# The second layer of a Strassen MLP: steps over four quads of units instead of two, with 1024-column splits

## The chip, the cores and the metric

The kernel runs on one core of a Trainium2 chip. Times are device microseconds of one execution. The engines are PE (matmuls), DVE, ACT and POOL (elementwise work) and SP, which issues most of the DMAs. Each engine works through its own queue in order.

## The reference, cut to what matters

Depth is one, so one Conformer convolution module and one squared-ReLU MLP are computed for 2048 tokens of width 1024, in float32:

```
h = rms_norm(x, mix_norm)
a, g = split(h @ w_in + b_in);  h = a * sigmoid(g)
h = causal_depthwise_conv_31(h) + conv_b
x = x + silu(layer_norm(h, ln_g, ln_b)) @ w_out + b_out
x = x + square(relu(rms_norm(x, mlp_norm) @ w1)) @ w2      # d_ff = 4096
```

## The kernel before

Activations lie transposed (features on partitions, 512 tokens to a tile), so there are four blocks of tokens. float32 products are made of three float32r matmuls: each operand is split into a high half (an ACT cast) and a low half (a DVE or POOL subtraction), and high by high, high by low and low by high are accumulated. "A split" below is this pair of instructions.

The first part of the program (up to some 1190 us) does the convolution of all blocks and the MLP of blocks 0 and 1. Nothing in it changes but the way one address of w2 is written. The second part, after `front.close()`, opens new pools and does blocks 2 and 3:

- *Projection* (`project_spilled`, twice 8 products of 24 matmuls): the convolution's output is read back from DRAM through the tiles of `loaded`, split, and multiplied by w_out; x2, the residual stream, goes to DRAM (`x2_pairs`).
- *First MLP layer* (class `Quad`). The two token blocks and the two halves of the weights make a 2 by 2 block product, done in Winograd's form of Strassen's scheme with 7 products instead of 8. The seven forms of the activations are B11, B21, T2, T1, T3, B22 and T4; the weights' are A11, A12, S2, S1, S3, S4 and A22. A quad is 2 x 128 hidden units for both blocks; there are 16. Its products are called P1, P2, P6, P5, P7, P3 and P4, 12 matmuls each. For the first twelve quads (`EARLY`) P1 and P2 run ahead, and their results wait in DRAM. After the squared ReLU POOL makes the seven forms that the second layer needs (four subtractions a quad, L785 to L788), and SP stores them (`keep`).
- *Second MLP layer* (L857 to L902). Outer loop: groups g of two quads (NG = 8); inner loop: two halves o of the output. One (g, o) is a half step: it loads two weight tiles of 512 KB (`raw_wq`), forms the seven weight forms in 512-column pieces (`blocks`, `w_split`), and does seven products of 12 matmuls on two pairs of PSUM banks (`both`). Each of the four finished results is a pair of tiles, 512 KB, added into x2 in DRAM by an accumulating DMA that POOL issues (L882). In the last group x2 is loaded instead, added, and stored to the output. `hidden(g)` loads and splits the hidden units of a group, 14 loads of 256 KB, once for both halves; the next group's call stands after the half o = 0.

Buffers that matter: 29 activation tiles (16 + 13) of 512 columns, high and low half, taken in turn; 6 weight splits of 512 columns (`N_WQ`); 5 load buffers (`N_LD`); 6 output tiles (`N_CC`); 4 raw weight tiles of 1024 columns; 4 pairs. The tile framework orders each engine's queue by itself, by priority and by what it expects to be ready; the code above sets program order and buffers only.

## Time and profile before

| | |
|---|---|
| three runs, median (lowest to highest) | 1991.04 us (1986.84 to 1992.85) |
| profiled execution: time, span | 1986.6, 1984.8 us |
| mean granted PE clock | 0.981 |
| busy: PE, PEld, DVE, ACT, POOL | 95%, 78%, 81%, 42%, 29% |
| DMA moved, mean rate | 303.15 MB, 153 GB/s |
| q0 (accumulating DMAs, issued by POOL) | 29.36 MB, 8.3% of 16 engines |
| q1 (all other DMAs, issued by SP) | 272.28 MB, 41.2% of 16 engines |

PE stands for the matmuls; their records overlap, so 95% doesn't mean that PE runs at its peak. PEld is the loading of weights into it. The share of a queue is the time that its packets took on the sixteen DMA engines.

### The profile page before, as it was taken

The numbers are of one execution on the slowest core, as the hardware profiler recorded it, in microseconds if no ns is written. First come the engines' busy times: TensorE is split into PE (matmuls) and PEld (weight loads), VectorE is DVE, ScalarE is ACT, GpSimd is POOL, SyncE is SP. The second block draws the span as 40 slices with busy tenths as digits, with TensorE's granted clock in tenths as the row PEclk, the third lists the DMA queues.
The fourth block names the chain that finished last, engine by engine and source line by source line (L and its number), as shares of the span: only waits on it lengthen the run. The fifth ranks groups of instructions, "written<-read, shape, count | busy, mean of one in ns | idle before, by whom it ended". The sixth has DMA issues, their size and how long they took to land.

```text
span 1984.8 us, 23561 instructions
## 1 busy us (share of the span) xinstructions
PE 1889.5 (95%) x8192; PEld 1544.2 (78%) x8192; DVE 1609.1 (81%) x2364; ACT 824.7 (42%) x1336; POOL 585.2 (29%) x387
## 2 busy tenths in 40 slices
PE   8999999999999999999999998999999998888897
PEld 6888888888778878788888876878888876766775
DVE  7999999999999999789999844785888586666653
ACT  5323225243453333443222424464445664555541
POOL 2256322644445630000000003402666421111113
PEclk9999999999999999999999998999999999999998
DMA  5223221432223333552221448856765598888875
GB/s 199 64 86 111 98 77 65 143 102 96 85 83 126 127 107 117 181 180 95 66 70 59 143 165 282 266 179 221 240 227 207 174 270 215 219 214 211 210 156 172
DMA packets 141623, 303.15 MB, mean 153 GB/s; under 512 B 13632, under 2 KB 40384, under 8 KB 141504
## 3 DMA queue, kind: packets, MB, share of 16 engines
q1 hardware_dynamic: 133440, 272.28, 41.2%
q0 software_dynamic: 8064, 29.36, 8.3%
q8 instruction: 64, 1.05, 0.2%
q14 instruction: 55, 0.45, 0.1%
HBM read 210.12 MB, written 91.47 MB: 152 GB/s over the span
## 4 chain that ended last, share of the span: by engine, by line
PE 39%; DMA 10%; DVE 5%; issue 3%; ACT 2%; POOL 0%; SPq 0%; DVEq 0%; ACTq 0%; POOLq 0%
PE ps L163 16%; PE px L609 11%; PE pz L609 5%; PE px L163 4%; DMA rawq<-in_w 4%; PE py L609 2%; DMA ld<-hB 2%; DMA ld<-hT 2%; DVE wq L585 1%; DVE act L93 1%; DMA c<-x 1%; ACT act L92 1%; ACT wq L584 0%; DMA x<-c 0%; DMA c<-conv 0%
## 5 line engine op out<-in xcount | busy, mean ns | idle before, releaser
L163 PE MATMUL ps<-act,w 128*128 128x512 f32 x2880 | 666.8, 392 | 10.2 <-ACT w L92 7.8
L163 PEld LDWEIGHTS ps<-act,w 128*128 128x128 f32 x2880 | 542.1, 189 | 126.7 <-ACT w L92 7.8
L163 PE MATMUL ps<-hid,w 128*128 128x512 f32 x1920 | 445.9, 392 | 6.2 <-DVE hid L93 5.8
L163 PEld LDWEIGHTS ps<-hid,w 128*128 128x128 f32 x1920 | 360.4, 189 | 86.8 <-DVE hid L93 8.6
L609 PE MATMUL px<-act,wq 128*128 128x512 f32 x1536 | 381.3, 402 | 44.1 <-DVE p L871 30.2
L609 PEld LDWEIGHTS px<-act,wq 128*128 128x128 f32 x1536 | 297.0, 195 | 114.5 <-DVE p L871 33.8
L352 DVE SCALAR_TENSOR_TENSOR cacc<-hc,cw,cacc 128x512 f32<-128x512 f32 x464 | 324.6, 748 | 1.4
L352 DVE SCALAR_TENSOR_TENSOR cacc<-h,cw,cacc 128x512 f32<-128x512 f32 x464 | 316.8, 747 | 0.0
L93 POOL TENSOR_TENSOR w<-raw,w 128x1024 fp32r<-128x1024 f32 x90 | 218.1, 2424 | 287.2 <-ACT w L92 281.3
L92 ACT CAST w<-raw 128x1024 fp32r<-128x1024 f32 (+1 forms) x150 | 155.1, 1035 | 289.3 <-PE ps L163 284.7
L609 PE MATMUL pz<-act,wq 128*128 128x512 f32 x768 | 186.7, 392 | 4.7 <-ACT p L828 2.8
L585 DVE TENSOR_TENSOR wq<-rawq,wq 128x512 fp32r<-128x512 f32 x144 | 116.3, 815 | 74.4 <-ACT wq L584 74.2
L609 PEld LDWEIGHTS pz<-act,wq 128*128 128x128 f32 x768 | 145.4, 190 | 36.0 <-ACT p L828 3.3
L584 ACT CAST wq<-rawq 128x512 fp32r<-128x512 f32 x192 | 117.8, 620 | 124.1 <-DMA rawq<-in_w_out 39.1
L585 POOL TENSOR_TENSOR wq<-rawq,wq 128x512 fp32r<-128x512 f32 x48 | 71.5, 1491 | 192.4 <-ACT wq L584 176.5
L440 DVE TENSOR_TENSOR h<-h,ps 128x512 f32<-128x512 f32 x128 | 86.9, 683 | 31.2 <-PE ps L163 29.5
L427 ACT ACTIVATE relu<-ps 128x512 f32<-128x512 f32 x64 | 38.2, 597 | 161.1 <-PE ps L163 160.9
L163 PE MATMUL px<-act,wq 128*128 128x512 f32 x384 | 90.2, 396 | 8.5 <-ACT act L92 7.9
L93 DVE TENSOR_TENSOR act<-ld,act 128x512 fp32r<-128x512 f32 x112 | 79.2, 726 | 23.5 <-ACT act L92 23.0
L609 PE MATMUL py<-act,wq 128*128 128x512 f32 x384 | 93.8, 392 | 2.9 <-DVE cc L697 2.9
L163 PEld LDWEIGHTS px<-act,wq 128*128 128x128 f32 x384 | 73.4, 192 | 24.8 <-ACT act L92 8.4
L882 POOL DMA_DIRECT2D x<-p x28 | 24.4, 872 | 230.3 <-DVE p L871 221.8
(133 smaller groups left out, 1816.7 us busy)
## 6 DMA issues: line engine op xcount, KB each, us to landing
raw<-in_w SPq DMA_DIRECT2D x104, 512.0 KB, 3.6
rawq<-in_w SPq DMA_DIRECT2D x76, 512.0 KB, 4.9
xt<-in_xT SPq DMA_DIRECT2D x64, 256.0 KB, 3.6
ld<-hT SPq DMA_DIRECT2D x64, 256.0 KB, 5.4
raw<-in_w_in SPq DMA_DIRECT2D x30, 512.0 KB, 3.2
x<-p POOLq DMA_DIRECT2D x28, 512.0 KB, 6.8
hB<-cc SPq DMA_DIRECT2D x48, 256.0 KB, 2.8
ld<-hB SPq DMA_DIRECT2D x48, 256.0 KB, 5.1
```

The costliest lines, as they stand in the source:

```text
L92: nc.scalar.copy(hl[:, 0, :], src)
L93: eng.tensor_sub(hl[:, 1, :], src, hl[:, 0, :].bitcast(F32))
L163: nc.tensor.matmul(ps, lhsT=w(k, a), rhs=x[:, b, :], start=k == 0 and i == 0, stop=k == len(xs) - 1 and i == 2,)
L352: nc.vector.scalar_tensor_tensor(out, h[:, k : k + T], cw[:, j, k : k + 1], acc, ALU.mult, ALU.add)
L427: nc.scalar.activation(r, ps, AF.Relu)
L440: nc.vector.tensor_add(x2[i][m], x2[i][m], ps)
L584: nc.scalar.copy(hl[:, 0, :], src)
L585: eng.tensor_sub(hl[:, 1, :], src, hl[:, 0, :].bitcast(F32))
L609: nc.tensor.matmul(ps, lhsT=hl[:, a, off + k * P : off + (k + 1) * P], rhs=x[:, b, :], start=first and k == 0 and i == 0, stop=k == n - 1 ...
L882: nc.gpsimd.dma_start(at, c, accum_op=ALU.add)
```

## The change

The second layer takes four quads a step, so there are 4 steps of two halves instead of 8. A product is 24 matmuls (`both` lists the four addresses in the weight tile), and the outputs are accumulated in DRAM after 3 steps instead of 7: 24 accumulating DMAs instead of 56. The forms of four quads lie together in DRAM (`hid_d`), so a load brings two quads, 512 KB; it is split as one tile of 1024 columns by one cast and one subtraction (`Split.add_pair`). A half step has four weight tiles, each split whole. Weight splits are all made by DVE. The buffers are cut anew: 14 activation pairs of twice the size, 2 weight splits of 1024 columns and 4 of 512, 3 load buffers ("in", which also hold C11 and P1 of a quad, `ca`) and 2 output tiles ("out"), 4 mid tiles and 2 sum tiles of 1024 columns. In the last step x2 is added when P1, P6, P5 and P4 are evicted (`kept`, `base`). The descriptor space of the accumulating DMAs is 4096 instead of 8192.

```diff
-N_WQ, N_LD, N_CC = 6, 5, 6
+N_LD = {"in": 3, "out": 2}
...
-    n_act = {"low": 16, "high": 13}
...
+    def act_pair(name="act"):
+
+        n = taken[0] % 14
         taken[0] += 1
...
+        side, pool_, bufs = ("high", high, 6) if n < 6 else ("low", low, 8)
+        return pool_.tile([P, 2, 2, T], F32R, name=name, tag=side, bufs=bufs)
+
+    class Split:
...
+        def add_pair(self, src):
+            t = act_pair()
+            self.pairs.append([t, 2])
+            nc.scalar.copy(t[:, 0], src)
+            nc.vector.tensor_sub(t[:, 1], src, t[:, 0].bitcast(F32))
...
     def mid_tile(name):
-        return mid.tile([P, T], F32, name=name, tag="m", bufs=6)
+        return mid.tile([P, T], F32, name=name, tag="m", bufs=4)
...
+    def w_split(src, eng=nc.vector):
+
+        n = src.shape[-1]
+        tag, bufs = ("wq", 2) if n == 2 * T else ("wh", 4)
+        hl = wts.tile([P, 2, n], F32R, name="w", tag=tag, bufs=bufs)
+        nc.scalar.copy(hl[:, 0, :n], src)
+        eng.tensor_sub(hl[:, 1, :n], src, hl[:, 0, :n].bitcast(F32))
         return hl
...
+    def sum_tile(name):
+        return mid.tile([P, 2 * T], F32, name=name, tag="s", bufs=2)
+
+    def wide(name, tag="out"):
+        return wts.tile([P, 2, T], F32, name=name, tag=tag, bufs=N_LD[tag])
...
-    hid_d = [{n: dram.tile([P, T], F32, name=f"h{n}_{q}") for n in form} for q in range(NQ)]
+    hid_d = [{n: dram.tile([P, 4, T], F32, name=f"h{n}_{g}") for n in form} for g in range(NQ // 4)]
...
         def p2(self):
             y = ybank()
-            product(y, w_split(self.a1[:, T:], nc.vector), form["B21"])
-            self.c11 = squared_relu(added(y, self.c1))
+            self.product(y, self.w12, "B21")
+            self.ca = wide("ca", "in")
+            self.c11 = squared_relu(added(y, self.c1, self.ca[:, 0, :]))
...
         def p3(self):
-            product(self.z, w_split(self.s4, nc.gpsimd), form["B22"], first=False)
-            self.c12 = squared_relu(added(self.z, self.u2))
+            self.product(self.z, self.ws4, "B22", first=False)
+            self.c12 = squared_relu(added(self.z, self.u2, self.cb[:, 1, :]))
...
     def hidden(g):
         out = {}
-        for n in (b for _, b in ORDER):
-            out[n] = [act_split(loaded(hid_d[2 * g + k][n])) for k in range(2)]
+        for n in ORDER:
+            s = Split()
+            for k in range(0, 4, 2):
+                s.add_pair(loaded(hid_d[g][n][:, k : k + 2, :]))
+            out[n] = s.parts()
         return out
 
     def blocks(g, o):
-        a1, a2 = [raw_wq(w2[g, o][:, 2 * i : 2 * i + 2]) for i in range(2)]
...
+        a11, a12, a21, a22 = [raw_wq(w2[g, o][:, i]) for i in range(4)]
+        s1, s2 = sum_tile("s1"), sum_tile("s2")
+        yield w_split(a11)
+        yield w_split(a12)
         nc.vector.tensor_add(s1, a21, a22)
         nc.vector.tensor_sub(s2, s1, a11)
-        out["S2"] = w_split(s2, nc.vector)
...
+            product(ps, w, hs, [k // 2 * T + i * 2 * P + k % 2 * P for k in range(4)], first)
...
+    steps = NG // 2
     h = hidden(0)
-    for g in range(NG):
+    for g in range(steps):
...
+            def out(x, n, t, ts=()):
+                for i, ps in enumerate(ts):
+                    nc.vector.tensor_add(t[:, i, :], ps, t[:, i, :])
                 if not end:
-                    nc.gpsimd.dma_start(at, c, accum_op=ALU.add)
+                    nc.gpsimd.dma_start(x2_pairs[n][2 * o + x], t, accum_op=ALU.add)
+                    return
...
             ws = blocks(g, o)
             px, py, pz = [[f() for _ in range(2)] for f in (xbank, ybank, zbank)]
-            both(px, "P1", h["B11"], ws["A11"])
-            p1 = copied(px, "p1")
...
+            w = [next(ws) for _ in range(3)]
+            both(px, h["B11"], w[0])
+            p1 = kept(px, "p1", 0, 0)
+            w.append(next(ws))
+            both(py, h["B21"], w[1])
+            out(0, 0, p1, py)
...
-    nc = bacc.Bacc("TRN2", target_bir_lowering=False, num_devices=1, dynamic_dma_scratch_size=8192)
+    nc = bacc.Bacc("TRN2", target_bir_lowering=False, num_devices=1, dynamic_dma_scratch_size=4096)
```

Three places of the queues. First SP at the start of the projection, where the first product's eight inputs (s, from conv_0) and the weights (rawq) are loaded; before:

```order
L590 DMA rawq<-in_w_out 128x1024
L598 DMA s<-conv_0_112 128x512
L598 DMA s<-conv_0_114 128x512
L598 DMA s<-conv_0_116 128x512
L598 DMA s<-conv_0_118 128x512
L598 DMA s<-conv_0_120 128x512
L590 DMA rawq<-in_w_out 128x1024
L598 DMA s<-conv_0_122 128x512
L598 DMA s<-conv_0_124 128x512
L598 DMA s<-conv_0_126 128x512
```

and with the change:

```order
L613 DMA rawq<-in_w_out 128x1024
L626 DMA s<-conv_0_112 128x512
L626 DMA s<-conv_0_114 128x512
L626 DMA s<-conv_0_116 128x512
L613 DMA rawq<-in_w_out 128x1024 x2
L626 DMA s<-conv_0_118 128x512
L626 DMA s<-conv_0_120 128x512
L626 DMA s<-conv_0_122 128x512
L613 DMA rawq<-in_w_out 128x1024
L626 DMA s<-conv_0_124 128x512
L626 DMA s<-conv_0_126 128x512
```

Three inputs instead of five stand ahead of the first wait for a buffer, and two weight tiles go between the third and the fourth.

Second, SP at the end of the first layer. The names hB and hT are the stored forms; with the change 10090 and 10091 are B11 and B21 of the first group, 10094 is T2, and 10111 to 10117 are the seven of the last group. Before, loads of the first quads' forms are already between the stores of quads 14 and 15:

```order
L598 DMA ld<-hT_0_10154 128x512
L712 DMA hB_14_10251<-cc 128x512
L598 DMA ld<-hT_1_10161 128x512
L598 DMA ld<-hT_0_10156 128x512
L598 DMA ld<-hT_1_10163 128x512
L590 DMA rawq<-in_w 128x1024
L598 DMA ld<-hB_0_10153 128x512
L712 DMA hT_14_10252<-h_12872 128x512
L712 DMA hT_14_10253<-h_12873 128x512
L712 DMA hT_14_10254<-cc 128x512
L712 DMA hB_15_10256<-cc 128x512
```

With the change T2 of the first group follows the last store of the last quad:

```order
L626 DMA ld<-hB_0_10090 128x1024
L626 DMA ld<-hB_0_10091 128x1024
L749 DMA hB_3_10113<-cb 128x512
L626 DMA ld<-hB_0_10091 128x1024
L749 DMA hT_3_10114<-h_12648 128x512
L749 DMA hB_3_10112<-ca 128x512
L749 DMA hT_3_10115<-h_12649 128x512
L749 DMA hT_3_10116<-cb 128x512
L749 DMA hT_3_10117<-h_12650 128x512
L626 DMA ld<-hT_0_10094 128x1024 x2
```

The loads have moved behind the stores that wait for POOL.

Third, DVE in a second half (o = 1) of the second layer, where act<-ld is a split of hidden units, w or wq one of a weight form, s a sum, and p, u are evictions. Before:

```order
L871 TENSOR_TENSOR p_14726<-py,p_14726 128x512
L93 TENSOR_TENSOR act<-ld,act 128x512 x2
L871 TENSOR_TENSOR p_14726<-py,p_14726 128x512
L585 TENSOR_TENSOR wq<-rawq,wq 128x512
L93 TENSOR_TENSOR act<-ld,act 128x512
L842 TENSOR_TENSOR s_15037<-rawq 128x512
L93 TENSOR_TENSOR act<-ld,act 128x512
L843 TENSOR_TENSOR s_15038<-s_15037,rawq 128x512
L585 TENSOR_TENSOR wq<-rawq,wq 128x512
L93 TENSOR_TENSOR act<-ld,act 128x512
L848 TENSOR_TENSOR rawq<-rawq,s_14825 128x512
```

With the change:

```order
L910 TENSOR_TENSOR rawq<-rawq,s_13045 128x1024
L573 TENSOR_TENSOR act<-ld,act 128x1024 x2
L608 TENSOR_TENSOR w<-s_13045,w 128x1024
L943 TENSOR_TENSOR p_13081<-py,p_13081 128x512
L573 TENSOR_TENSOR act<-ld,act 128x1024
L943 TENSOR_TENSOR p_13081<-py,p_13081 128x512
L573 TENSOR_TENSOR act<-ld,act 128x1024
L608 TENSOR_TENSOR w<-s_13044,w 128x1024
L573 TENSOR_TENSOR act<-ld,act 128x1024 x2
L608 TENSOR_TENSOR w<-rawq,w 128x1024
L573 TENSOR_TENSOR act<-ld,act 128x1024 x2
```

Each split covers 1024 columns, and two splits of hidden units stand ahead of each weight split.

## Rows read from the trace of the kernel before

**Rows 1.** Windows, 1198 to 1976 us: busy us and instructions of each engine, clock, DMA share, GB/s.

```profile
1198.00:1290.00 92.00, 91.05 (x395) 74.95 (x396) 55.72 (x78) 43.81 (x75) 42.02 (x30) 0.97 0.84 277
1290.00:1340.00 50.00, 47.13 (x211) 38.55 (x210) 43.35 (x78) 34.16 (x62) 2.70 (x2) 1.00 0.54 180
1340.00:1594.00 254.00, 254.00 (x1122) 210.08 (x1120) 186.10 (x213) 133.88 (x227) 137.23 (x92) 1.00 0.64 214
1594.00:1603.20 9.20, 7.30 (x26) 5.78 (x26) 6.66 (x11) 7.20 (x14) 0.00 (x0) 0.81 0.96 321
1603.20:1975.80 372.60, 325.68 (x1345) 261.93 (x1343) 231.84 (x365) 181.76 (x329) 68.59 (x70) 0.94 0.81 206
```

**Rows 2.** PE timeline: start us, us, engine line op tiles xcount [idle before <-releaser].

```profile
1198.36 0.80 PE L163 MATMUL px<-act,wq 128*128 128x512 f32 x1 [7.94 <-ACT act L92]
...
1600.45 5.60 PE L609 MATMUL px<-act,wq 128*128 128x512 f32 x24
...
1973.03 2.88 PE L609 MATMUL px<-act,wq 128*128 128x512 f32 x12
```

**Rows 3.** Lines by form, 1606 to 1985 us: count | busy us, mean ns | idle before.

```profile
L609 PE MATMUL px<-act,wq 128*128 128x512 f32 x757 | 196.7, 415 | 44.1 <-DVE p L871 30.2 <-ACT p L828 4.9 <-DVE c L873 4.7
...
L609 PE MATMUL pz<-act,wq 128*128 128x512 f32 x384 | 92.8, 390 | 2.8 <-ACT p L828 2.8
```

**Rows 4.** Chain of waits, 1600 to 1985 us: start us, us, what.

```profile
1680.63 2.72 PE py L609 x12
...
1751.28 10.47 DMA rawq<-in_w
...
1797.35 11.63 DMA rawq<-in_w
```

**Rows 5.** Queues and issues, 1600 to 1985 us: packets, MB, share; count, KB, us to landing.

```profile
q0 software_dynamic: 8064, 29.36, 42.9%
q1 hardware_dynamic: 21904, 49.57, 37.6%
...
rawq<-in_w SPq DMA_DIRECT2D x29, 512.0 KB, 7.3
x<-p POOLq DMA_DIRECT2D x28, 512.0 KB, 6.8
ld<-hT SPq DMA_DIRECT2D x54, 256.0 KB, 5.7
...
c<-x SPq DMA_DIRECT2D x8, 512.0 KB, 4.2
```

**Rows 6.** Instructions of tile ld, 1600 us to the end.

```profile
DMA to landing us min/median/max: 2.5/6.1/11.9
```

**Rows 7.** DVE and ACT timelines near 1148 us, splits of 1024 columns.

```profile
1148.48 1.23 DVE L93 TENSOR_TENSOR w<-raw,w 128x1024 fp32r<-128x1024 f32 x1 [0.94 <-ACT w L92]
...
1147.41 1.04 ACT L92 CAST w<-raw 128x1024 fp32r<-128x1024 f32 x1
```

**Rows 8.** SP and ACT timelines at the hand-over.

```profile
1192.03 2.66 SPq L598 DMA_DIRECT2D s<-conv  x5
...
1199.72 1.52 SPq L598 DMA_DIRECT2D s<-conv  x3
...
1202.41 1.27 ACT L92 CAST act<-s 128x512 fp32r<-128x512 f32 x2
```

**Rows 9.** Lines of POOL (1350 to 1600 us) and of DVE (1350 to 1550 us).

```profile
L585 POOL TENSOR_TENSOR wq<-rawq,wq 128x512 fp32r<-128x512 f32 x32 | 48.7, 1521 | 98.0 <-ACT wq L584 85.2 <-DMA p<-p 6.5 <-DVE cc L697 4.1
L788 POOL TENSOR_TENSOR h<-cc,h 128x512 f32<-128x512 f32 x15 | 25.1, 1672 | 9.6 <-DVE s L723 6.2 <-ACT cc L702 1.6 <-DVE wq L585 1.2
...
L585 DVE TENSOR_TENSOR wq<-rawq,wq 128x512 fp32r<-128x512 f32 x20 | 24.9, 1251 | 11.8 <-ACT wq L584 11.8
```

**Rows 10.** Chain of waits, the last 11 us.

```profile
1973.98 4.64 DMA c<-x
1978.74 0.69 DVE c L873
```

More of the change, by code (lines that the diff above doesn't have):

```diff
@@ L627, in load_plain @@
         raw = raw_wq(src)
-        hl = [w_split(raw[:, h * T : (h + 1) * T], (nc.vector, nc.gpsimd)[h]) for h in range(2)]
-        return lambda k, a: hl[k // 4][:, a, k % 4 * P : (k % 4 + 1) * P]
+        hl = w_split(raw)
+        return lambda k, a: hl[:, a, k * P : (k + 1) * P]
     def project_spilled(b, ss, norm, w0=None):
@@ L649, in conformer_mlp @@
     HK = KD // 2
-    form = {n: [None] * HK for n in ("B11", "B21", "B22", "T1", "T2", "T3", "T4")}
+    form = {n: Split() for n in ("B11", "B21", "B22", "T1", "T2", "T3", "T4")}
     n0 = [None] * HK
@@ L709, in __init__, with kept, product @@
             self.q, self.early = q, False
+        def kept(self, n):
+            return hid_d[self.q // 4][n][:, self.q % 4, :]
         def keep(self, n, t):
-            nc.sync.dma_start(hid_d[self.q][n], t)
+            nc.sync.dma_start(self.kept(n), t)
+        def product(self, ps, half, n, first=True):
+            w, off = half
+            product(ps, w, form[n].parts(), [off + k for k in IN_ORDER], first)
         def high(self):
@@ L842, in blocks @@
         nc.vector.tensor_add(s1, a21, a22)
         nc.vector.tensor_sub(s2, s1, a11)
-        out["S2"] = w_split(s2, nc.vector)
-        out["S1"] = w_split(s1, nc.vector)
+        yield w_split(s2)
         nc.vector.tensor_sub(a21, a11, a21)
-        out["S3"] = w_split(a21, nc.vector)
+        yield w_split(s1)
         nc.vector.tensor_sub(a12, a12, s2)
-        out["S4"] = w_split(a12, nc.vector)
-        out["A22"] = w_split(a22, nc.vector)
-        return out
-    def both(tiles, name, hs, w, first=True):
+        yield w_split(a21)
@@ L854, in both, with base, kept @@
+        yield w_split(a12)
+        yield w_split(a22)
+    def both(tiles, hs, w, first=True):
         for i, ps in enumerate(tiles):
-            product(ps, w, hs, off=i * 2 * P, first=first)
+            product(ps, w, hs, [k // 2 * T + i * 2 * P + k % 2 * P for k in range(4)], first)
+    steps = NG // 2
     h = hidden(0)
-    for g in range(NG):
+    for g in range(steps):
+        end = g == steps - 1
         for o in range(2):
-            end = g == NG - 1
-            def out(x, n, ts, t):
-                at = x2_pairs[n][2 * o + x]
-                if end:
-                    base = pair("c")
-                    nc.sync.dma_start(base, at)
-                c = t if t is not None and not end else pair("c")
+            def base(x, n):
+                t = wide("x2")
+                nc.sync.dma_start(t, x2_pairs[n][2 * o + x])
+                return t
+            def kept(ts, name, x, n):
+                t = pair(name)
+                x2 = base(x, n) if end else None
@@ L895, in conformer_mlp @@
-            out(1, 1, px, p5)
-            both(pz, "P3", h["B22"], ws["S4"], first=False)
-            out(0, 1, pz, u2)
-            both(px, "P4", h["T4"], ws["A22"], first=False)
-            out(1, 0, px, None)
-            if o == 0 and g < NG - 1:
+            w = [next(ws) for _ in range(3)]
[4 more added lines that the diff above has]
+            out(0, 0, p1, py)
+            w.append(next(ws))
@@ new lines, in conformer_mlp @@
+            both(px, h["T2"], w[2], first=False)
+            u2 = kept(px, "u2", 0, 1)
+            w.append(next(ws))
+            both(pz, h["T1"], w[3])
+            p5 = kept(pz, "p5", 1, 1)
+            w.append(next(ws))
+            both(px, h["T3"], w[4], first=False)
+            out(1, 1, p5, px)
+            both(pz, h["B22"], w[5], first=False)
+            out(0, 1, u2, pz)
+            both(px, h["T4"], w[6], first=False)
+            out(1, 0, kept(px, "c", 1, 0))
+            if o == 0 and not end:
```

162 lines of the change are left out of this document (85 added, 77 removed).

## The prediction

> **What bounds the kernel now.** I read the windows by stage first. From 1340 to 1594 us, inside the first MLP layer, PE is busy in every microsecond at full clock; in the second layer, 1603.2 to 1975.8 us, the granted clock is 0.94 and the DMA engines are busy 0.81 of the time [rows 1]. The limits of that stage come from the PE timeline: P1 begins after the first 12 of the 24 matmuls at 1600.45, and 12 matmuls that begin at 1973.03 end it [rows 2]. It holds 1344 matmuls, and the chain shows 12 in 2.72 us, 226.7 ns each [rows 4]: 304.7 us of work in 372.6, so 68 us are lost. By the lines, PE stands idle 44.1 us before px matmuls and 2.8 before pz, 47 together [rows 3]; the other 21 are matmuls at a lower clock, 0.45 us for each idle one. Nothing of this size is lost elsewhere behind 1198: only 7.94 us before the first px matmul, where the front half hands over [rows 2].
>
> What ends the waits is read from the chain: weight tiles (rawq) that land after 10.47 and 11.63 us, step after step [rows 4]. The reason is in the queue table of this stage (a window of 384.8 us): q0, the accumulating DMAs, moves 29.36 MB, which is 56 transfers of 0.524 MB, and takes 42.9% of the sixteen engines, 165 us or 2.95 us each; q1 moves 49.57 MB in 37.6%, 145 us, so 0.524 MB cost 1.53 us [rows 5]. One half step (12 matmuls times 7 products, 19.0 us of PE) asks for two weight tiles, 3.5 tile equivalents of hidden units and four accumulations: 5.5 x 1.53 + 4 x 2.95 = 20.2 us. The stage is bound by its transfers, not by PE.
>
> **The change, part by part.**
>
> *Accumulations.* A half step is now 24 matmuls times 7, 38.1 us of PE, with still four accumulations, 24 in all instead of 56. Demand over a whole step of two halves: 8 weight tiles and 14 hidden tiles, 22 x 1.53 = 33.7, and 8 x 2.95 = 23.6, together 57 us in 76.2. The transfers stop being the bound on average, and PE becomes it. All 68 us could go.
>
> *What is late next: the hidden tiles.* Fourteen tile pairs hold exactly one step; before, 29 tiles held two steps of 14. So a form's pair is overwritten only when the second half step has used it, and nearly all loads of a step fall into that half: some 10 of the 14 with 4 to 5 weight tiles and four accumulations, 14.5 x 1.53 + 11.8 = 34 us in 38.1, a share of 0.89. They pass through three load buffers. One buffer is held from the issue until the low half is subtracted: the landing L, a cast of 1.04 us and a subtraction of 1.23 [rows 7]. Two loads per product and three buffers give a pace of (L + 2.3) x 2/3 a product, against 5.44 for PE: no cost up to L = 5.9. The nearest rows for L: 4.2 us for 512 KB where nothing accumulates, 7.3 for 512 KB weight tiles beside the accumulations, 5.7 for 256 KB [rows 5], and up to 11.9 for one ld [rows 6]. I take 7.3, the same size in the same traffic: pace 6.4, 0.96 us lost in each of 6 products (the first form is loaded in the half before) of 3 second halves, 17 us. Bounds: 0 at 4.2, and 73 at 11.9 (14.2 x 2/3 - 5.44 = 4.0 for each of 18 products).
>
> The rows say that 512 KB land in 4.2 to 7.3 us. [...] The Trainium skill (Trainium Kernel Development and Optimization, section Best Practices) also advises to double-buffer so that DMA and compute overlap, which speaks against giving up the second set of tiles; the pace above is what that costs here.
>
> *Engine queues in the second half.* DVE per half: 7 weight splits, up to 14 hidden splits and 4 sums, 25 x 1.23 = 31, and 6 additions of 0.68 (a DVE addition from PSUM is 0.69 [rows 10]), 4: 35 of 38.1 us, in order. A weight split waits for its buffer (two of 1024 columns), released when the product two before has ended, and stands behind two hidden splits: 1.04 + 3 x 1.23 = 4.7 us, under 5.44. It costs nothing while the tiles have landed; if they are late, it is part of the pace above. POOL only issues DMAs here, and SP needs 0.5 us per issue [rows 8], some 22 in 76 us. Half of the evictions' adds and copies go; PE hid them and hides them now. The smaller descriptor space costs nothing either: even if each accumulation had to land (6.8 us [rows 5]) before the next is issued, four would fit in 38.
>
> *Start of the second layer.* Before, the first quads' forms were queued ahead of the last units' stores. Now T2 stands on SP behind the last unit's T4 store, which needs four POOL subtractions of 1.67 us [rows 9] after P3 of that unit. With P4 of it ending at 0: subtractions from -0.6 to 6.1, T2 issued at 6.2, landed at 13.5 (L = 7.3), split by 15.8; P6 wants it at 10.9, and the other forms and the next weight tile are queued behind it. 5 us; bounds 2 (L = 4.2) and 9 (11.9). Before, this place lost time too, 9.2 us for 36 matmuls of 8.2 at a clock of 0.81 [rows 1]; I leave that 1 us aside.
>
> *Clock and ends.* (17 + 5) x 0.45 = 10 us; 2 us for the base loads of the last step. Second layer: 304.7 + 17 + 5 + 10 + 2 = 339, a gain of 34.
>
> *Tail.* The last chain was a base load of 4.64 us for a tile that is freed late, then the addition at 1978.74 [rows 10]. Now the base is loaded ahead and added in the eviction: 3.5 us less (bounds 2 and 5).
>
> *Handover and projection.* The inputs s pass through 3 buffers instead of 5. Five were issued at once, the rest at 1199.72 and cast at 1202.41 [rows 8], a trip of 2.7 us. Now the fourth, fifth and sixth go where the sixth did, and the seventh and eighth wait for another split, 2.7 + 0.6 + 0.7 later: product 0 of the projection ends about 4 us later than it did. The second input is queued one store later: 1.5 us. Together +5.5; bounds 1 and 13 (the same for both inputs, with the clock).
>
> *First layer.* 32 POOL splits of 1.52 us become DVE work, at most 1.25 us each there [rows 9], 40 us on top of DVE's 186 in 254 [rows 1]: 226, still under PE. Nothing, bounds -3 and +6 (what PE loses in 1290 to 1340 now, 50 less 47.1, and twice that). The 1024-wide splits, wider tiles for ca and cb and fewer mid tiles lie under the same cover; without it each split would cost 1.04 + 1.23.
>
> **Sum:** 5.5 - 34 - 3.5 = -32. The profiled execution took 1986.6 (span 1984.8): 1954.6. It stands at the low end of the runs (1986.8 to 1992.9); against the median of 1991.0 it is **1959 us**.
>
> **Rivals.**
>
> A, everything hidden: L stays under 5.9 because a step has half the accumulations. Then the layer takes 304.7 + 5 x 1.45 + 2 = 314, the sum is -57, and the time 1934. For it: 4.2 us where nothing accumulates. Against: a share of 0.89 in the second halves, as high as now. [...] Chance 0.17.
>
> B, weight tiles late: all four rawq tiles belong to one half step, so the last tile of the next half is issued only when the fifth product has ended and its split is done, 3.6 us later; landing, two sums, two hidden splits and a weight split (L + 6.2) must fit into the 12.7 us that three products (16.3) then leave: L up to 6.5; in a half without hidden splits up to 7.8. At 10.5, as the chain has it, 4.0 us are lost in three halves and 2.7 in four, 23 x 1.45 = 33 beside the forecast: 1992 at worst, 1975 at half of it. For: those very waits lead the chain now. Against: fewer transfers. Chance 0.18.
>
> C, slower: the three load buffers set the pace in full. With tail and projection the gain is used up when the layer takes 371, 57 more than A's: 39 us of idle over 18 products, 2.2 each, a pace of 7.6, L = 9.1. From there on it is slower; at L = 10, 8.2 a product, 2.76 x 18 x 1.45 = 72 on A's 314, sum +15, 2006 us. For: ld landings up to 11.9 us. Against: a median of 6.1. Chance 0.11.
>
> **How the numbers follow.** Forecast 0.50 (1948 to 1970), A 0.17, B 0.18, C 0.11, and 0.04 for a sum that cancels to nothing. The likeliest gives 1959. The range, 1931 to 1986, holds the forecast, B nearly whole and most of A, and leaves out C and the no-change case. 0.3% (6 us) is about what a measurement can tell from no change: faster 0.84, same 0.05, slower 0.11.
>
> **What would show it.** q0 with 24 transfers and some 70 us; the second layer near 339 us and its DMA share near 0.65; idle PE mostly in second halves, ended by ld landings of about 7 us; some 4 us more at the first projection; no PE idle in the first layer's loops. I am wrong if the loop before 1594 loses time, if waits for rawq lead the chain again, or if first and second halves are equally long.

## The result and the profile after

The change makes the kernel faster: 1963.12 us, median of four runs (1961.10 to 1966.95), against 1991.94 beside it on the same chip. The ratio is 0.9861, 95% interval 0.9834 to 0.9887. The profiled execution took 1964.58 us (span 1962.8, mean granted clock 0.986). All stage lengths below come from profiled executions; from one to the other the change is -22 us, since the profiled execution before, 1986.6 us, is faster than any of the four timed ones (1986.84 to 1994.58).

The windows by stage of the kernel after (columns as in [rows 1]): projection, first layer, second layer.

```profile
1198.00:1298.60 100.60, 95.15 (x394) 76.18 (x395) 56.42 (x75) 40.09 (x57) 22.99 (x14) 0.94 0.75 242
1298.60:1619.70 321.10, 311.61 (x1355) 253.23 (x1354) 213.50 (x290) 163.15 (x253) 86.11 (x62) 0.99 0.61 200
1619.70:1958.30 338.60, 317.45 (x1346) 256.90 (x1344) 204.21 (x200) 138.49 (x161) 28.03 (x28) 0.96 0.69 191
```

| stage | before, us | after, us | difference | predicted |
|---|---|---|---|---|
| projection, from 1198 | 92.0 | 100.6 | +8.6 | +5.5 |
| first layer | 313.2 | 321.1 | +7.9 | 0 |
| second layer | 372.6 | 338.6 | -34.0 | -34 |
| tail | 9.0 | 4.5 | -4.5 | -3.5 |

The column before follows [rows 1] and [rows 2] (the first layer there is 1290 to 1603.2). The differences add up to -22.0, where the prediction's sum is -32. In the second layer PE idles 338.6 less 317.45, 21 us, instead of 47, and the matmuls take 317.45 instead of 325.68.

The queues of the kernel after, 1600 to 1963 us (columns as in [rows 5]):

```profile
q1 hardware_dynamic: 17427, 56.11, 46.9%
q0 software_dynamic: 3456, 12.58, 20.8%
...
ld<-hT SPq DMA_DIRECT2D x32, 512.0 KB, 5.7
rawq<-in_w SPq DMA_DIRECT2D x29, 512.0 KB, 5.7
...
x<-p POOLq DMA_DIRECT2D x12, 512.0 KB, 8.7
```

24 accumulations are left, 20.8% of 363 us, 75 us of the sixteen engines instead of 165. Weight tiles land in 5.7 us instead of 7.3. The instructions of tile ld give the spread of the loads of hidden units, against [rows 6]:

```profile
DMA to landing us min/median/max: 3.6/5.6/10.6
```

What is left of the waits stands in few places. The PE timeline of the kernel after (columns as in [rows 2]), start of the layer, then all waits over 1 us in it:

```profile
1616.98 4.54 PE L634 MATMUL px<-act,w 128*128 128x512 f32 x19
...
1638.72 0.79 PE L634 MATMUL px<-act,w 128*128 128x512 f32 x1 [6.22 <-ACT act L572]
...
1678.44 8.02 PE L634 MATMUL py<-act,w 128*128 128x512 f32 x22 [3.63 <-DVE w L608]
...
1721.70 1.09 PE L634 MATMUL py<-act,w 128*128 128x512 f32 x2 [2.51 <-ACT w L607]
...
1804.08 1.22 PE L634 MATMUL py<-act,w 128*128 128x512 f32 x2 [2.81 <-ACT w L607]
...
1886.64 0.73 PE L634 MATMUL py<-act,w 128*128 128x512 f32 x2 [2.49 <-ACT w L607]
```

The first is P6 of the first half step, behind the split of T2; the other four are P2 (tile py), each behind a weight split: in the second half of step 0, and in the first halves of steps 1, 2 and 3. But for the wait in step 0, second halves are not where time goes: from step 0 to step 3 they take 44.7, 38.8, 38.1 and 38.1 us, first halves 49.1, 42.9, 45.3 and 41.6. The windows of the second half of step 2 and the first half of step 3:

```profile
1840.50:1878.60 38.10, 38.10 (x170) 31.55 (x169) 29.13 (x28) 23.57 (x27) 3.46 (x4) 1.00 0.86 245
1878.60:1920.20 41.60, 38.59 (x169) 31.33 (x168) 26.91 (x29) 9.75 (x10) 0.86 (x1) 1.00 0.60 175
```

At a DMA share of 0.86 this second half runs in 38.1 us, which is its bare work (168 matmuls at 226.7 ns). Who makes P2 late is told by the chain of waits of the kernel after (start us, us, what):

```profile
1663.59 9.95 DMA rawq<-in_w
...
1673.63 1.24 DVE s L905
...
1677.25 1.15 DVE w L608
...
1706.90 1.06 ACT act L572
...
1709.24 9.85 DMA ld<-hT
...
1719.41 0.88 DVE act L573
...
1721.76 1.16 DVE w L608
...
1722.96 2.07 PE py L634 x4
```

In step 0 the split for P2 (A12) stands on DVE behind the sums, and the first sum (L905) waits for the fourth weight tile, 9.95 us on its way. At the end of a second half it stands on ACT and DVE behind the splits of T4, the last of the fourteen loads, issued at 1709.24 when a load buffer came free and 9.85 us on its way. The cast of A12 follows it on ACT, 7 us after P4 ended at 1713.5 (ACT timeline of the kernel after):

```profile
1720.60 1.05 ACT L607 CAST w<-rawq 128x1024 fp32r<-128x1024 f32 x1
```

The sum waits in the same place there, as the DVE timeline of the kernel after shows:

```profile
1717.01 1.23 DVE L905 TENSOR_TENSOR s<-rawq 128x1024 f32<-128x1024 f32 x1 [3.17 <-DMA rawq<-in_w]
```

At the start of the layer T2 is late because the stores ahead of it wait for POOL. P4 of the last unit ends at 1619.70; POOL's first subtraction waits for a squared ReLU on ACT, which stands behind casts of the first loads of hidden units, the second of which is waited for until 1622.2. POOL and SP timelines of the kernel after:

```profile
1624.55 1.29 POOL L845 TENSOR_TENSOR h<-cb,ca 128x512 f32<-128x512 f32 x1 [12.93 <-ACT cb L736]
...
1632.12 12.30 SPq L626 DMA_DIRECT2D ld<-hT  x6
```

The tail: after the last matmuls one addition and the store are left, where a base load stood in [rows 10]. The last pieces of the chain of the kernel after:

```profile
1953.01 5.45 PE px L634 x24
...
1958.48 0.69 DVE c L936
```

**Projection.** The handover cost what it did, 7.50 us before the first px matmul instead of 7.94 [rows 2]. The new time is at the second input. SP timelines: before, its first load goes out at 1225, behind the fourth store of x2,

```profile
1225.06 0.57 SPq L598 DMA_DIRECT2D s<-conv  x1
```

and with the change 11 us later, behind the sixth:

```profile
1236.07 0.42 SPq L626 DMA_DIRECT2D s<-conv  x1
1240.28 0.32 SPq L626 DMA_DIRECT2D s<-conv  x1
```

PE then waits for it near 1250 (PE timeline of the kernel after), 3.1 us in all:

```profile
1249.01 0.50 PE L163 MATMUL px<-act,w 128*128 128x512 f32 x1 [1.90 <-ACT act L92]
1249.73 0.96 PE L163 MATMUL px<-act,w 128*128 128x512 f32 x3 [0.22 <-DVE act L93]
1251.63 0.80 PE L163 MATMUL px<-act,w 128*128 128x512 f32 x1 [0.93 <-ACT act L92]
```

Of the 8.6 us, 4.5 are idle PE (5.45 against 0.95) and 4.1 are matmuls at a lower clock: 0.94 in this stage, 0.97 before.

**First layer.** PE idles 9.5 us (321.1 less 311.61) instead of 4.8 [rows 1]; its matmuls take 3.2 us more. PE's waits of the kernel after, 1340 to 1605 us (waited for, us in total, times, longest):

```profile
PE pz L634 <- DVE p L731: 3.6, 8, 0.8
PE py L634 <- DVE ca L731: 2.8, 1, 2.8
```

The one of 2.8 us is an eviction of P2 near 1345 behind the splits of the second normalisation on DVE. The eight before P3 have another reason, in the DVE lines of the kernel after, 1350 to 1600 us (count | busy us, mean ns | idle before):

```profile
L768 DVE TENSOR_TENSOR s<-rawq 128x512 f32<-128x512 f32 x16 | 14.1, 883 | 36.7 <-DMA rawq<-in_w 36.7
...
L769 DVE TENSOR_TENSOR s<-s,rawq 128x512 f32<-128x512 f32 x16 | 11.0, 690 | 0.4
```

Before most quads' sums DVE waits some 3 us for a weight tile, and the evictions that PE needs stand behind. In the kernel before the same sum hardly waited (same view and window):

```profile
L722 DVE TENSOR_TENSOR s<-rawq 128x512 f32<-128x512 f32 x15 | 14.3, 951 | 1.9 <-DMA rawq<-in_w 1.9
```

That is 3.6 of the 9.5 idle us. 5.4 stand ahead of 1350, the 2.8 among them.

### The profile page after: what moved, and what is told of

The parts are those of the page before. It is cut to its first block, busy times and chain, and to the rows that moved or that the text cites. A ratio compares the mean times of both kernels' runs of the same rounds, so it can differ in the third digit from the quotient of the medians.

```text
span 1962.8 us, 22587 instructions
## 1 busy us (share of the span) xinstructions
PE 1888.2 (96%) x8192; PEld 1539.0 (78%) x8192; DVE 1555.3 (79%) x2184; ACT 765.1 (39%) x1100; POOL 468.6 (24%) x295
## 4 chain that ended last, share of the span: by engine, by line
PE 37%; DMA 9%; DVE 7%; issue 4%; ACT 2%; POOL 1%; SPq 0%; DVEq 0%; ACTq 0%; POOLq 0%
PE ps L163 16%; PE px L634 10%; PE pz L634 5%; PE py L634 4%; PE px L163 3%; DMA rawq<-in_w 3%; DMA ld<-hT 3%; DVE w L608 1%; DMA conv<-c 1%; DVE act L573 1%; DMA rawq<-in_w_out 1%; DVE act L93 1%; DMA x<-x 1%; DMA conv<-s 0%; ACT w L607 0%
## 5 line engine op out<-in xcount | busy, mean ns | idle before, releaser
L634 PE MATMUL px<-act,w 128*128 128x512 f32 x1536 | 365.3, 392 | 9.5 <-ACT act L572 6.2
L634 PEld LDWEIGHTS px<-act,w 128*128 128x128 f32 x1536 | 289.7, 189 | 73.8 <-ACT act L572 6.6
L634 PE MATMUL pz<-act,w 128*128 128x512 f32 x768 | 183.1, 390 | 4.5 <-DVE p L731 3.6
L607 ACT CAST w<-rawq 128x1024 fp32r<-128x1024 f32 (+1 forms) x120 | 105.1, 877 | 186.7 <-PE px L634 77.6
L634 PEld LDWEIGHTS pz<-act,w 128*128 128x128 f32 x768 | 143.4, 188 | 38.0 <-ACT w L607 6.7
L608 DVE TENSOR_TENSOR w<-rawq,w 128x1024 fp32r<-128x1024 f32 (+1 forms) x120 | 124.6, 1039 | 39.2 <-ACT w L607 38.4
L634 PE MATMUL py<-act,w 128*128 128x512 f32 x384 | 100.5, 413 | 16.6 <-ACT w L607 7.8
L573 DVE TENSOR_TENSOR act<-ld,act 128x1024 fp32r<-128x1024 f32 x56 | 68.3, 1229 | 51.5 <-ACT act L572 50.8
L634 PEld LDWEIGHTS py<-act,w 128*128 128x128 f32 x384 | 76.0, 200 | 37.4 <-ACT w L607 9.1
L163 PE MATMUL px<-act,w 128*128 128x512 f32 x384 | 93.2, 402 | 12.0 <-ACT act L92 10.3
L163 PEld LDWEIGHTS px<-act,w 128*128 128x128 f32 x384 | 74.0, 194 | 30.8 <-ACT act L92 12.6
L572 ACT CAST act<-ld 128x1024 fp32r<-128x1024 f32 x56 | 58.9, 1052 | 78.5 <-DMA ld<-hT 38.6
```

The costliest lines, as they stand in the source:

```text
L163: nc.tensor.matmul(ps, lhsT=w(k, a), rhs=x[:, b, :], start=k == 0 and i == 0, stop=k == len(xs) - 1 and i == 2,)
L572: nc.scalar.copy(t[:, 0], src)
L573: nc.vector.tensor_sub(t[:, 1], src, t[:, 0].bitcast(F32))
L607: nc.scalar.copy(hl[:, 0, :n], src)
L608: eng.tensor_sub(hl[:, 1, :n], src, hl[:, 0, :n].bitcast(F32))
L634: nc.tensor.matmul(ps, lhsT=hl[:, a, off : off + P], rhs=x[:, b, :], start=first and k == 0 and i == 0, stop=k == n - 1 and i == 2, skip_g ...
```

## The experiments

In the order in which they ran. "Layer" is the second layer in the profiled execution, from the first matmul of P1 to the end of the last product; "starts" is where it starts (both to within 0.2 us). A single run has no interval. Four runs with the first layer of the kernel after and an edit in the second only (double_acc, no_t4, no_both, narrow_loads) start the layer at 1620.7 to 1626.4 instead of 1619.7, so a start that differs by less than some 7 us says nothing by itself.

| run | time, us | ratio to before, 95% | layer starts | layer, us |
|---|---|---|---|---|
| before | 1986.6 (profiled) | | 1603.2 | 372.6 |
| after | 1963.12 | 0.9861 [0.9834, 0.9887] | 1619.7 | 338.6 |
| half_acc | 1949.23 (one run) | | 1601.8 | 336.8 |
| double_acc | 1989.64 (one run) | | 1622.0 | 361.3 |
| no_t4 | 1954.35 (one run) | | 1620.7 | 327.7 |
| no_both | 1945.37 (one run) | | 1626.4 | 313.0 |
| s_wide | 1962.37 | 0.9856 [0.9841, 0.9871] | 1622.0 | 336.1 |
| wh5 | 1975.90 | 0.9923 [0.9906, 0.9939] | 1634.6 | 335.2 |
| wq4 | 1946.75 | 0.9778 [0.9763, 0.9793] | 1624.5 | 313.3 |
| in4 | 1956.06 | 0.9829 [0.9804, 0.9854] | 1623.5 | 324.8 |
| wq4_in4 | 1943.87 | 0.9769 [0.9753, 0.9785] | 1625.4 | 312.6 |
| pool_back | 1970.08 | 0.9901 [0.9878, 0.9925] | 1628.3 | 332.2 |
| narrow_loads | 1964.25 | 0.9870 [0.9850, 0.9890] | 1622.6 | 335.3 |
| wq4_raw5 | 1956.35 | 0.9830 [0.9816, 0.9843] | 1631.0 | 317.2 |

The four single runs shared one run of the kernel before, 1986.82 us.

**Half as many accumulations, alone.** In the kernel before, only the odd ones of the first seven steps (g = 1, 3, 5) accumulate, so the output lacks the other sums; nothing else changes.

```diff
-                if not end:
+                if not end and g % 2:
                     nc.gpsimd.dma_start(at, c, accum_op=ALU.add)
```

> The kernel before, but the second layer accumulates into x2 only for the odd groups g = 1, 3, 5 (the results of g = 0, 2, 4, 6 are left out of the output): 24 accumulating DMAs as after the change, with 256 KB loads, 512-column splits, two quads a step and all buffers as before. Theory T (the second layer was bound by its transfers, the accumulations above all): a half step asks for 5.5 x 1.53 + 1.7 x 2.95 = 13.4 us of transfers against 19 of PE, so the layer falls from 372.6 us to 320 to 345, the time to about 1940 to 1960. Rival R (the look-ahead of the weight tiles, freed late by DVE, was the bound, and the number of accumulations is beside the point): the layer stays over 360.

1949.23 us, 37.6 less than before on the same chip. The layer's window and queue row of this run:

```profile
1601.80:1938.60 336.80, 317.51 (x1345) 257.00 (x1343) 232.30 (x367) 186.56 (x331) 41.21 (x38) 0.97 0.65 179
```

```profile
q0 software_dynamic: 3456, 12.58, 20.6%
```

This one condition gives the second layer all that the whole change gives it (336.8 against 338.6 us), with 256 KB loads, 512-column splits and steps of two quads. 32 accumulations less save 35.8 us, 1.1 us each. In time this run is even 14 us below the kernel after: its second layer starts 17.9 us earlier, because the projection and the first layer are those of the kernel before.

**Twice as many, in the new kernel.** Each accumulating DMA is issued twice, the second time to another address.

```diff
                     nc.gpsimd.dma_start(x2_pairs[n][2 * o + x], t, accum_op=ALU.add)
+                    nc.gpsimd.dma_start(x2_pairs[n][(2 * o + x + 2) % 4], t, accum_op=ALU.add)
```

> The changed kernel with each accumulation of the second layer issued twice, the second time into another pair of x2 (the output is changed by that): 48 accumulating DMAs. Theory T: a second half asks for 34 + 12 = 46 us of transfers against 38 of PE, a first half for about 30, so the three second halves grow by 8 to 15 us each and the time by 25 to 45 us. Rival R: under 8 us more.

1989.64 us, the whole gain is gone. The window of the layer and two of its waits in the PE timeline of this run:

```profile
1622.00:1983.30 361.30, 325.48 (x1346) 260.31 (x1344) 204.57 (x200) 138.09 (x161) 48.44 (x52) 0.94 0.81 213
```

```profile
1732.15 8.69 PE L634 MATMUL py<-act,w 128*128 128x512 f32 x24 [7.22 <-ACT w L607]
...
1909.43 8.78 PE L634 MATMUL py<-act,w 128*128 128x512 f32 x24 [6.58 <-ACT w L607]
```

Clock and DMA share are back at 0.94 and 0.81, the values of [rows 1]. The added transfers are paid for where P2 waits: 2.5 to 3.6 us each become 4.5 to 7.2. The sum, 26.5 us more than the kernel after, is in the range expected, the place isn't: the second halves of steps 0 to 2 grow by some 2 to 4 us each, not 8 to 15, and the first halves of steps 1 and 3 by 6 to 7. Both directions agree, so the number of accumulations is what moved the second layer. That an accumulation holds its pair of tiles until it has landed is not how it costs: in the kernel before, 1600 to 1985 us, ACT and DVE wait 6.2 us for such landings in all, and PE never.

**The waits before P2.** Two runs on the kernel after: no_t4 leaves out the loads of T4 from the second step on (its splits take B22's tile instead), no_both leaves out the fourth weight tile as well (A12 is used for it).

```diff
+                if g and n == "T4":
+                    s.add_pair(b22[k // 2][0][:, 0].bitcast(F32))
+                else:
+                    s.add_pair(loaded(hid_d[g][n][:, k : k + 2, :]))
...
-        a11, a12, a21, a22 = [raw_wq(w2[g, o][:, i]) for i in range(4)]
+        a11, a12, a21 = [raw_wq(w2[g, o][:, i]) for i in range(3)]
+        a22 = a12
```

> The changed kernel without the DMA loads of form T4 for steps 1 to 3 (its split is made from B22's tile instead; the same casts and subtractions in the same place). In the changed kernel P2 of the first half of steps 1, 2 and 3 waits 2.7, 3.5 and 3.0 us, 9.2 together, for the split of A12. Theory Q (that split stands behind T4's splits, whose load is late): the 9.2 us go. Rival S (the two sums ahead of it on DVE wait for the fourth weight tile): they stay. If both waits lie side by side: at least 2 us stay in each.

> The changed kernel without T4's loads (as in no_t4) and without the load of the fourth weight tile of each half step (A12's tile takes its place in the sums and in the last product). By Q, by S and by both side by side the waits before P2 of steps 1 to 3 go, from 9.2 us to under 1.5; about 12 us less in all with the clock. If they stay, the cause is another, such as the two buffers of the weight splits.

Without T4's loads the waits before P2 are 3.03, 3.28, 1.45 and 0.39 us and are ended by DVE; in step 0, where T4 is still loaded, little changes, in step 1 all of the wait stays, and in steps 2 and 3 most of it goes, so the 2 us that were to stay in each did not. Without the weight tile too, none of them is left. The PE timeline of no_both has one wait over 1 us in the whole layer:

```profile
1642.08 0.50 PE L634 MATMUL px<-act,w 128*128 128x512 f32 x1 [3.76 <-ACT act L572]
```

Two waits lay side by side before P2; in step 1 taking one away only shows the other. These runs also move fewer bytes, so the 25.6 us that the layer is shorter are not those of the waits alone; the run with the splits in halves, further down, settles that.

**A wider ring for the projection's inputs.** Two inputs s share one load buffer, so six can be in flight.

```diff
-            ss.add(loaded(conv_out[j][i], "s"))
+            if j % 2 == 0:
+                t = wide("s", "in")
+            nc.sync.dma_start(t[:, j % 2, :], conv_out[j][i])
+            ss.add(t[:, j % 2, :])
```

> The changed kernel, with the inputs s of both projections loaded two to a load buffer (the buffers are 1024 columns wide, an s fills half), so six of the eight inputs can be under way instead of three. In the changed kernel the projection ends 8.7 us later than before, with waits of 1.90, 0.22 and 0.93 us in the first product on the second input and a low clock behind them. Theory P (three load buffers): these waits go, and the projection is 4 to 9 us shorter; time -4 to -9 us. Rival (weight splits wholly on DVE, or the clock by itself, make it longer): under 2 us.

No difference from the kernel after. The SP timeline of this run says why: the second input's loads still go out at the same place of SP's queue, 1235.76 instead of 1236.07, and PE waits 2.4 us near 1250 instead of 3.3 (for the input itself 1.3 instead of 3.1; a wait for POOL grows from 0.2 to 1.1).

```profile
1235.76 0.92 SPq L717 DMA_DIRECT2D s<-conv  x2
```

So the number of buffers is not what makes the second input late. Its place in SP's queue stayed as it was; that this is the reason is read from the timeline, and no run moved it.

**A fifth buffer for half-width weights.** wh goes from 4 to 5; the row tiles of the later norms get one buffer instead of two for it.

```diff
-        tag, bufs = ("wq", 2) if n == 2 * T else ("wh", 4)
+        tag, bufs = ("wq", 2) if n == 2 * T else ("wh", 5)
...
```

> The changed kernel with five instead of four 512-column weight buffers (room comes from three tiny statistics tiles with one buffer instead of two). In the first layer's loop P3 now waits 0.2 to 0.6 us in every quad for the addition that evicts P5, which stands on DVE behind sums that wait some 3 us for their second weight tile. Theory H (that tile is freed late because the split that empties it waits for a buffer until P3 ends): the sums no longer wait, the waits go, time -3 to -6 us. Rival X (DVE has too much to do since POOL's splits moved to it): nothing changes, within 2 us.

12 us slower than the kernel after, all of it in the first layer: the second starts 15 us later. The tile framework, given a buffer more, puts the sums a step earlier on DVE, ahead of the eviction of P6. The DVE timeline and PE's waits, 1340 to 1605 us, of this run:

```profile
1452.86 0.69 DVE L770 TENSOR_TENSOR s<-rawq 128x512 f32<-128x512 f32 x1 [5.93 <-DMA rawq<-in_w]
1453.47 0.68 DVE L733 TENSOR_TENSOR u<-px,ca 128x512 f32<-128x512 f32 x1
```

```profile
PE px L636 <- DVE u L733: 8.2, 7, 2.1
```

From 1350 to 1600 DVE waits 60 us for weight tiles instead of 37, and P7 waits for u behind it. The row tiles alone are not the cause: the run with a fourth load buffer, below, gives them up too, and its second layer starts 3.8 us later, not 15.

**The weight splits of A12, S1 and S4 in halves.** They go to the four half-width buffers, which the second layer doesn't use otherwise; the other splits keep the two wide ones.

```diff
+    class Halves:
+        def __init__(self, src):
+            self.t = [w_split(src[:, i * T : (i + 1) * T]) for i in range(2)]
...
-        yield w_split(a12)
+        yield w_halves(a12)
...
-        yield w_split(s1)
+        yield w_halves(s1)
...
-        yield w_split(a12)
+        yield w_halves(a12)
```

> The changed kernel, where the second layer makes every second weight split as two of 512 columns in the four buffers that only the first layer uses, so four splits of 1024 columns can be held instead of two. Theory Q/S (what delays P2 at the start of a half is the place of A12's split in the queues, since it can begin only when P4 of the half before has ended and late loads stand ahead by then): with two more buffers it is made a product earlier, the waits of some 13 us shrink to under 4, time -8 to -15 us. Rival (the loads themselves are late, whatever the order): within 4 us.

16 us faster than the kernel after, with the same loads and accumulations. The window of the layer and the only wait over 1 us in it (PE timeline) of this run:

```profile
1624.50:1937.80 313.30, 307.61 (x1345) 253.30 (x1344) 203.18 (x221) 137.24 (x181) 27.77 (x28) 0.99 0.73 205
```

```profile
1639.91 0.80 PE L634 MATMUL px<-act,w 128*128 128x512 f32 x1 [4.32 <-ACT act L572]
```

The layer is 313 us, as short as with the loads left out (no_both). The DVE and PE timelines of this run show A12's second half split at 1698.14, ahead of T4's splits, and P2 of step 1 beginning 16 us later:

```profile
1698.14 0.68 DVE L608 TENSOR_TENSOR w<-rawq,w 128x512 fp32r<-128x512 f32 x1
...
1714.80 5.60 PE L634 MATMUL py<-act,w 128*128 128x512 f32 x24
```

So the late tiles were no lack of transfer. The loads land no sooner than in the kernel after (median 5.9 us for hidden units and 6.2 for weight tiles, against 5.6 and 5.8). The split for P2 was made too late, since it had to wait for one of two wide buffers until P4 had ended; with buffers of its own it is made some three products ahead. That the pieces are only half as wide can't be the reason, as they are ready so long before. Weight tiles are then also asked for sooner: DVE's sums wait 5.6 us for them in the layer instead of 21.7. Of the 25 us that the layer gains, 4.8 are lost ahead of it, where a wait of 2.91 us stands before the last P3 (0.55 in the kernel after); that is within the scatter of the starts.

**A fourth load buffer.** The row tiles of the later norms get one buffer instead of two for it, as with the fifth half-width buffer.

```diff
-N_LD = {"in": 3, "out": 2}
+N_LD = {"in": 4, "out": 2}
...
```

> The changed kernel with four load buffers instead of three (room as in wh5). By the pace (L + 2.3) x 2/3 of three buffers and the measured landing of 5.6 us (5.3 us a product, under 5.44) a fourth gives nothing inside the second halves; it brings T4's last load forward, which leaves the wait for the fourth weight tile, and helps the projections: -3 to -8 us. If the three buffers held back the second layer more than the waits show: -10 us or more.

1956.06 us, 7 less than the kernel after, but the intervals of the two ratios overlap, so the gain is not clear of noise. In the profiled execution the layer is 13.8 us shorter. The wait of P6 at the start of the layer is gone (6.22 us in the kernel after), but 3.14 us before a pz product stand near there now, and P2 of the later steps still waits 3.38, 1.01 and 1.16 us.

**Both of them.**

> Both edits that helped by themselves: the weight splits of A12, S1 and S4 in halves of 512 columns (their own buffers, so that four stand ahead of the product instead of two), and a fourth load buffer. Theory S (the two kinds of wait in the second layer, behind the weight sums and behind the last unit's stores, are separate ones): the gains of 16 and 7 us add as far as idle PE is left, 1940 us (1936 to 1944), second layer 305 to 311 us, no wait above 1.5 us in it. Theory O (the split in halves already took the waits that the fourth buffer takes): 1945 to 1950, no different from the split in halves alone.

1943.87 us; its interval overlaps that of the splits in halves alone, and the layer, 312.6 us, is under 1 us shorter. The time is just inside theory S's range (1936 to 1944) and just under O's (1945 to 1950), so it doesn't decide. The layer does, for O: it is not 305 to 311 us, and waits of 1.57 and 2.29 us are left in it. What the fourth buffer takes from the layer, the splits in halves have mostly taken already. It is the shortest time measured in this study, 0.9% under the kernel after by the two ratios.

**The first layer's splits back on POOL.**

```diff
-            self.ws4 = w_split(self.s4), 0
-            self.w22 = w_split(self.a2[:, T:]), 0
+            self.ws4 = w_split(self.s4, nc.gpsimd), 0
+            self.w22 = w_split(self.a2[:, T:], nc.gpsimd), 0
```

> The splits of S4 and A22 in the first layer go back from DVE to POOL, 32 of them; the rest of the DVE order in the loop is as it was, and the second layer is the same. Theory F1 (the moved splits are what the first layer lost: DVE's evictions stand behind them, and behind a wait for a weight tile that they release late): the waits of PE before P3, 3.6 us from 1345 to 1605, vanish, 1957 to 1961 us. Theory F2 (the waits come from the sums that stand ahead of the eviction in DVE's queue and wait for a weight tile, whoever makes the splits): the waits before P3 stay or grow, since DVE's subtractions slow down again beside POOL's (0.69 us to 1.0 or more), 1962 to 1968 us.

1970.08 us, and F1 falls. PE's waits, 1300 to 1605 us, of this run:

```profile
PE pz L634 <- DVE p L731: 10.7, 9, 1.8
```

With 32 splits less on DVE the waits before P3 grow from 3.6 to 10.7 us, and DVE waits 47.9 us for weight tiles instead of 36.7. F2 holds in that the splits on DVE are not the cause; the time is 2 us above its range, and its interval just overlaps that of the kernel after. The slower subtractions that F2 named as well came only in part: L769 stays at 690 ns.

**The loads of hidden units in two pieces of 256 KB.**

```diff
-        nc.sync.dma_start(t, src)
+        if len(src.shape) == 2:
+            nc.sync.dma_start(t, src)
+        else:
+            for i in range(2):
+                nc.sync.dma_start(t[:, i, :], src[:, i, :])
```

> The 512 KB loads of hidden units in the second layer become two loads of 256 KB each into the same tile; the splits stay 1024 columns wide. My theory: the size of a load carries nothing, since the layer's time is in the accumulations and in the waits before P2; 48 more issues of 0.5 us on SP fit into its idle time: 1960 to 1967 us. Rival (fewer and larger loads are part of the gain): 56 more transfers cost their fixed share and SP issues late, at least 0.5 us of each on the path to P2: over 1970 us. Rival (two halves land on more engines at once and so sooner): below 1958.

No difference: 1964.25 us, and the layer takes 335.3 us. The size of the load carries nothing here.

**A fifth raw weight tile.** Beside the splits in halves; the row tiles of the later norms get one buffer instead of two here too.

```diff
-        t = top.tile([P, 2 * T], F32, name="rawq", tag="rawq", bufs=4)
+        t = top.tile([P, 2 * T], F32, name="rawq", tag="rawq", bufs=5)
...
```

> The split in halves as before, and a fifth buffer for raw weight tiles (the norms' row tiles of the second part get one buffer instead of two for it). In the DVE queue of the first layer the three sums then stand one step earlier, ahead of P6's eviction u, as they do in the run with five half-width weight buffers. Theory F2 (DVE's evictions are late because the sums ahead of them wait for a weight tile): with a tile more in flight DVE's wait for rawq from 1350 to 1600, 37 us, falls below 12, PE's waits before P3 (3.2 us) vanish, and the time is 4 to 8 us under the split in halves, 1939 to 1943 us. Rival F3 (the place of the sums in the queue is itself the cost, whenever the tile lands): PE waits for u or p again, 8 us or more as with the five buffers, 1954 to 1960 us.

Neither theory was met in full. DVE still waits 40.6 us for weight tiles, since the sums moved up by as much as the tile did; PE waits for the eviction behind them (PE's waits, 1300 to 1625 us, of this run):

```profile
PE px L636 <- DVE u L733: 6.4, 8, 1.0
```

It is 9.6 us slower than the splits in halves alone, and the second layer starts 6.5 us later, which the scatter of the starts could give alone. F3 named the place, but its 8 us of waits are 6.4. As the wait for the tile and the place in the queue came together again, this run doesn't tell them apart. A first layer with the sums kept behind the evictions wasn't tried; that it would give the 7.9 us back is open.

## Why the prediction was right, and where it wasn't

The forecast was 1959 us with a range of 1931 to 1986; it came to 1963.12. Step by step:

- **The bound.** Right. The transfers bound the second layer through the accumulations: taking 32 of 56 away in the kernel before gave -35.8 us there, doubling them in the kernel after took 22.7 back. The price per accumulation was right as well: 20.8% of 363 us over 24 is 3.1 us of the sixteen engines against 2.95.
- **The second layer, 339 us.** 338.6 came out, and 21 us of idle PE against 22 plus the 2 of the ends, but the term that made most of it failed: the 17 us for the ring of three load buffers in second halves. L was 5.6 us, not 7.3, so that the pace, (5.6 + 2.3) x 2/3 = 5.3, stayed under 5.44, as rival A had it; second halves run nearly free. In its place came rival B's place of trouble, the split for P2 behind late weight tiles and the last T4 load: 3.63, 2.51, 2.81 and 2.49 us, 11.4 in all. The ring has a share in these, though not by the pace: T4's last load goes out only when a load buffer comes free, and with a fourth buffer the layer was 13.8 us shorter (in4). The sentence "it costs nothing while the tiles have landed; if they are late, it is part of the pace above" is the step that failed: the two wide weight buffers were a limit of their own, and wq4 shows what they cost, 25 us of the layer and 16 of the time. The two prices don't add (wq4_in4). That the sum met the time is luck of two sizes.
- **Rival A** is what the layer becomes once this limit is gone: 314 us predicted, 313.3 measured in wq4.
- **Start of the layer**, 5 us: 6.22 measured, behind T2 as said, but the size is luck. T2 went out 12.4 us after the end of P4, not 6.2, because POOL began 4.9 us after it instead of 0.6 before; it landed in 5.5 us instead of 7.3, and P6 itself was due later.
- **Clock.** 10 us were put beside 22 of idle; the matmuls took 317.45 against 304.7 us of work, 12.7 beside 21.2. The ratio of 0.45 was a little low, 0.60 here.
- **Tail.** -3.5 predicted, -4.5 measured: the base load is gone whole.
- **Handover and projection.** +5.5 predicted, +8.6 measured, and in another place. Product 0 was to lose 4 us to the ring of three; it lost about 1 (55 matmuls in the 16 us from 1198 instead of 58, and a wait of 0.37). The second input was to lose 1.5 us for a store ahead of it; it stood behind two, and lost 3 us of PE and the clock after them.
- **First layer.** 0 predicted, +7.9 measured, over the upper bound of 6. The step "226, still under PE. Nothing" counted DVE's busy time (it even fell, to 160 us in 255) and not its queue: an eviction behind a sum that waits for a weight tile is late however idle the engine is. That accounts for 3.6 us of idle PE; the rest is ahead of 1350 and in the clock. pool_back shows that the moved splits themselves aren't it; why the tile comes later than before stays open.
- **Its signs of being wrong.** The first came true: the first layer's loop loses time. The second did in part: waits for weight tiles stand in the chain again, beside T4's load. The third did not: the halves differ, though it is the first ones that are longer, and the forecast had put the idle time into second halves. The sum over profiled executions was 10 us short of the forecast: 8 in the first layer and 3 in the projection, less 1 in the tail.

Of the 56 loads of 512 KB that SP issues here the quickest took 3.6 us and the median 5.6; ahead of the second layer, in the kernel before, 30 loads of that size (raw<-in_w_in) took a median of 3.2 us. The Trainium skill (DMA: Bandwidth & Descriptors, section Anatomy of one DMA) has a fit for DMAs that POOL issues, which gives an estimate of 3.2 us for 512 KB; the trace does not agree for the accumulating DMAs that POOL issues here, whose medians are 7.1 to 8.7 us.

## What to carry to other kernels

Before rebuilding a stage to save transfers, price each kind of transfer by the engine time of its queue and try the smallest edit that removes the dear kind: here one condition showed that the accumulations were the whole gain. Then go through each buffer that the rebuilt stage shares, because the next bound was not bandwidth but a split that waited for one of two buffers, with a ring of three load buffers beside it. In queues worked off in order, ask of each waiting instruction what stands behind it, also in stages that the change only grazes, and read the order anew after any change of a buffer's count: one buffer more made the first layer 15 us longer in one run and, less surely, 6 in another.

## What the runs showed that was not expected

- An accumulating DMA of 512 KB takes 2.9 to 3.1 us of the sixteen engines in three runs (half_acc, after and double_acc: 20.6% of 348 us over 24, 20.8% of 363 over 24, 35.6% of 388 over 48), about twice a plain one of that size [rows 5], yet PE lost only 1.1 and 0.9 us for each (35.8 us over 32, 22.7 over 24).
- DVE's 512-column subtractions beside a busy POOL: L723 and L724 before are L769 and L770 after, 1276 and 1017 ns against 690 and 683, with POOL busy 137 us before and 76 after, 1350 to 1600 us. POOL's share does not foretell it: in pool_back POOL is busy 124 us in this window and the two stay at 690 and 683; in wq4_raw5 it is busy 80, and the first of them (L771 there) takes 1208. What does was not tested.
